# First weight chunk in pieces of one k-tile, with the transposed input beside the weights

## The chip, the cores and the metric

The kernel runs on one core of a Trainium2 chip. The metric is the device time of one execution in microseconds (us), lower is better. Every time below is from runs of the kernel before the change or from the trace of one profiled execution of it.

## What is computed

One hybrid layer on an input `x` of 256 rows by 1024 columns in float32: a gated feed-forward block, a mixer (causal depthwise convolution beside attention over 16 heads), and a second gated feed-forward block. The change touches the beginning of the first block alone:

```
def rms_norm(x, g):
    xf = x.astype(jnp.float32)
    y = xf * lax.rsqrt(jnp.mean(xf * xf, axis=-1, keepdims=True) + EPS)
    return (y * g.astype(jnp.float32)).astype(x.dtype)

def swiglu(h, w_gate, w_up, w_down):
    return (jax.nn.silu(h @ w_gate) * (h @ w_up)) @ w_down

    x = x + 0.5 * swiglu(rms_norm(x, ffn1_norm), ffn1_w_gate, ffn1_w_up, ffn1_w_down)
```

## The kernel before, in words

Every product `h @ w` is cut into chunks of 512 columns of `w` (256 for the last columns). A chunk has 8 k-tiles: 128 rows of `w` each, against 128 features of `h`. The method `gemm` does one chunk. It loads pieces of up to two k-tiles into `raw` (a ring of 5 tiles), and for each piece ScalarE (ACT) writes `hi`, the weights rounded to a type that TensorE (PE) multiplies in one pass, and VectorE (DVE) writes `lo`, the rest that the rounding left. The activations exist in the same two halves, `hTh` and `hTl`. For each k-tile and each of the two halves `t` of the rows there are then three matmuls of 128x512: `hi` by `hTh`, `lo` by `hTh`, `hi` by `hTl`. So one chunk is 8 x 2 x 3 = 48 matmuls, which add up in two PSUM banks `acc` (a ring of 3 banks).

The first block's `ffn` takes chunks in pairs: chunk one is gate columns (`g`), chunk two the up columns (`u`) that belong to them. `sg`, the silu of `g`, and `av`, the product of `sg` and `u`, need the reciprocal root of the mean of squares, `rs`. It is applied after the product, so that the matmuls need only `x` transposed times the gain, which is what `hTh` and `hTl` hold.

In the first chunk the function `start` loads `x` transposed (`x0` with the gains for k-tile 0, `xT` for the others, in pieces of 1, 2, 2 and 2 k-tiles) in turn with the weight pieces (1, 1, 2, 2 and 2 k-tiles). ACT makes `hTh`, DVE makes `hTl`, and GpSimd (POOL) squares each k-tile of `xT` and adds the squares into `sq`. After the chunk PE adds `sq` over the partitions (`tr<-ones,sq`), DVE makes `ms` of it, and POOL `rs`. After chunk two `load_rest` issues the loads of the constants `cst` and of `x` in its natural layout, which is first read at 166 us.

All loads are issued by one queue, SyncE's (SP), in program order. A load into a `raw` tile waits until `lo` of the piece that lay there before is written, and all loads behind it wait too. The order of instructions on each engine is fixed when the program is built; each engine works through its own list and waits at semaphores. Two more PSUM tiles, `cv`, are used before the change by the convolution alone, in the middle of the kernel.

Of the kernel before, what the change touches and what calls it, by code (L numbers as in the profile page):

```python
# [17 lines left out]
P = 128  # L18
# [26 lines left out]
class Build:  # L45
# [14 lines left out]
    def acc(self):  # L60
        return self.ps.tile([P, CH], F32, tag="acc", name="acc", bufs=3)

    def tr(self):
        return self.ps.tile([P, CH], F32, tag="tr", name="tr", bufs=3)
# [31 lines left out]

    def gemm(self, w, c, n, kt, ah, al, pump=0, pool=0.0, first=False, split_k=None,
             side=None, before=None):

# [8 lines left out]
        for kp in sizes:  # L108
            ahead = before(k0) if before is not None else None
# [3 lines left out]
            with self.tc.issue_after(ahead.ins) if ahead else nullcontext():  # L113
                self.last_dma = nc.sync.dma_start(
                    raw[:, : kp * n].rearrange("p (k n) -> p k n", n=n), w(c, k0, kp)
                )
            step = 1 if first else 2
            for s in range(0, kp, step):
                e = min(s + step, kp)
                self.share += pool  # L120
                pool_lo = self.share >= 1.0
                if pool_lo:
                    self.share -= 1.0
                self.split(
                    raw[:, s * n : e * n], hi[:, s * n : e * n], lo[:, s * n : e * n], pool_lo
                )
            for t in range(2):
# [83 lines left out]

    def ffn(self, wgu, wd, hT, rstd_of, x, emit, tail=None, before=None, after=None):

# [8 lines left out]
        for i, n in enumerate(widths):  # L222
            last = i == len(widths) - 1
            if not last:
                if before is not None and i == 0:
                    g = self.gemm(
                        wgu, c, n, KD, ah, al, first=True, split_k=(1, 1), before=before
                    )
                else:
                    g = self.gemm(wgu, c, n, KD, ah, al)  # L230
                c += 1
                if rstd is None:
# [8 lines left out]
                u = self.gemm(wgu, c, n, KD, ah, al)  # L241
                c += 1
                if i == 0 and after is not None:
                    after()
# [54 lines left out]
    def conv(self, uT, tiles):  # L299
# [3 lines left out]
        for c0 in tiles:  # L303
            accs = [self.ps.tile([P, S], F32, tag="cv", name="cv", bufs=2) for _ in range(2)]
            for j in range(TAPS - 1, -1, -1):
# [195 lines left out]
    def run(self):  # L501
        nc, tc, io = self.nc, self.tc, self.io
        cst = self.cst = self.const.tile([P, C_ALL], F32, name="cst")
        x = self.big("x")
        xT = self.big("xT")
        hTh, hTl = self.big("hTh", F32R), self.big("hTl", F32R)

        def w_of(name, kt, n_of=lambda c: CH, off_of=None):
            t = io[name]

            def f(c, k0, kp):
                n = n_of(c)
                base = c * P * kt * CH
                a = t[base : base + P * kt * n].rearrange("(p k n) -> p k n", p=P, n=n)
                return a[:, k0 : k0 + kp, :]

            return f
# [7 lines left out]
        for _ in range(WARM):  # L525
            nc.tensor.matmul(wps[:, :P], idle, idle, start=True, stop=True)
        xT_d = io["xT"]

        sq = self.big("sq")
        self.ones = self.const.tile([P, 2], F32, name="ones")  # L530
        nc.vector.memset(self.ones, 1.0)

        def start(k0):

            if k0 == 0:
                dma = nc.sync.dma_start(x0, io["x0"])
                ks = (0,)
            elif k0 == 1:
                dma = nc.sync.dma_start(xT[:, S : 2 * S], xT_d[:, S : 2 * S])
                ks = (1,)  # L540
            else:
                sl = slice(k0 * S, (k0 + 2) * S)
                dma = nc.sync.dma_start(xT[:, sl], xT_d[:, sl])
                ks = (k0, k0 + 1)
            for j in ks:
                g = x0[:, j : j + 1]
                sl = slice(j * S, (j + 1) * S)
                src = xT[:, sl] if j else x0[:, KD:]
                nc.gpsimd.tensor_tensor(sq[:, sl], src, src, ALU.mult)
                if j:  # L550
                    nc.gpsimd.tensor_tensor(sq[:, :S], sq[:, :S], sq[:, sl], ALU.add)
                nc.scalar.activation(hTh[:, sl], src, AF.Copy, scale=g)
                nc.vector.scalar_tensor_tensor(
                    hTl[:, sl], src, g, hTh[:, sl].bitcast(F32), ALU.mult, ALU.subtract
                )
            return dma

        x0 = self.const.tile([P, KD + S], F32, name="x0")
# [8 lines left out]
        def ss_tile(name):  # L567
            return self.tmp.tile([P, 4], F32, tag="ss", name=name, bufs=2)

        def rstd_x():  # L570

            sums = self.tr()
            for t in range(2):
                nc.tensor.matmul(
                    sums[:, t : t + 1], sq[:, t * P : (t + 1) * P], self.ones[:, :1],
                    start=True, stop=True,
                )
            return self.rsqrt_mean(sums[:, :2], D, 2)

        def load_rest():  # L580
            with tc.issue_after(self.last_dma.ins):
                nc.sync.dma_start(cst, io["cst"])
# [10 lines left out]
        def emit_into(dst, src):  # L593
# [6 lines left out]

        self.ffn(
            w_of("w1gu", KD), w_of("w1d", KF), (hTh, hTl), rstd_x, x, emit_into(x1, x),
            self.residual_T(x1, ss1, h1h, h1l, C_GM), before=start, after=load_rest,
        )
# [209 lines left out]
```

## Time and profile before

| | |
|---|---|
| time, median of 3 runs | 655.03 us (653.30 to 655.46) |
| time of the profiled execution | 653.98 us |
| span in its trace | 652.2 us, so 1.8 us lie around it |
| PE busy | 640.5 us, 98% of the span |
| DVE busy, ACT busy | 413.1 us (63%), 342.6 us (53%) |
| matmuls in the trace | 2956 |

The span runs from the first instruction to the last one in the trace. A busy share says how much of the span an engine had work under way; for PE the ends of matmuls are modelled, so it can be busy and yet slow. Times inside the kernel are counted from the start of the span.

### The profile page before, as it was taken

The numbers are of one execution on the slowest core, as the hardware profiler recorded it, in microseconds if no ns is written. First come the engines' busy times: TensorE is split into PE (matmuls) and PEld (weight loads), VectorE is DVE, ScalarE is ACT, GpSimd is POOL, SyncE is SP. The second block draws the span as 40 slices with busy tenths as digits, with TensorE's granted clock in tenths as the row PEclk, the third lists the DMA queues.
The fourth block names the chain that finished last, engine by engine and source line by source line (L and its number), as shares of the span: only waits on it lengthen the run. The fifth ranks groups of instructions, "written<-read, shape, count | busy, mean of one in ns | idle before, by whom it ended". The sixth has DMA issues, their size and how long they took to land.

```text
span 652.2 us, 8131 instructions
## 1 busy us (share of the span) xinstructions
PE 640.5 (98%) x2956; PEld 519.8 (80%) x2956; DVE 413.1 (63%) x664; ACT 342.6 (53%) x512; POOL 132.5 (20%) x80
## 2 busy tenths in 40 slices
PE   7999999999999999999999999999999999999997
PEld 5788888888888888877777777788888888888886
DVE  5764636455532399999989874775754546455541
ACT  5543545354534645668665685943654535454330
POOL 6300000000025667847744400000000000000000
PEclk8999999999999999999999999999999999999999
DMA  8865655647565556444454433365655666656740
GB/s 275 315 224 164 193 193 173 216 132 233 163 213 163 183 175 219 144 153 134 156 162 130 162 124 102 130 207 179 197 171 182 193 194 182 189 162 204 206 124 32
DMA packets 33000, 114.98 MB, mean 176 GB/s; under 512 B 3648, under 2 KB 5056, under 8 KB 32960
## 3 DMA queue, kind: packets, MB, share of 16 engines
q1 hardware_dynamic: 32960, 114.46, 54.8%
q8 instruction: 23, 0.38, 0.3%
q14 instruction: 17, 0.14, 0.1%
HBM read 113.40 MB, written 1.05 MB: 175 GB/s over the span
## 4 chain that ended last, share of the span: by engine, by line
PE 90%; DVE 3%; ACT 3%; DMA 1%; issue 1%; SPq 0%; DVEq 0%; ACTq 0%
PE acc L134 28%; PE acc L133 28%; PE acc L135 28%; PE tr L178 2%; PE tr L423 1%; DMA raw<-w1gu 1%; PE tr L481 1%; DVE cv L317 1%; DVE lo L93 1%; ACT hi L91 1%; PE tr L466 1%; ACT gate L686 1%; ACT pr L445 0%; DVE hxn L385 0%; PE tr L397 0%
## 5 line engine op out<-in xcount | busy, mean ns | idle before, releaser
L91 ACT CAST hi<-raw 128x1024 fp32r<-128x1024 f32 (+1 forms) x216 | 222.9, 1037 | 242.1 <-PE acc L135 217.3
L93 DVE TENSOR_TENSOR lo<-raw,hi 128x1024 fp32r<-128x1024 f32 (+1 forms) x174 | 217.2, 1253 | 182.1 <-ACT hi L91 177.2
L93 POOL TENSOR_TENSOR lo<-raw,hi 128x1024 fp32r<-128x1024 f32 x42 | 100.9, 2421 | 219.4 <-ACT hi L91 219.2
L317 DVE SCALAR_TENSOR_TENSOR cv<-uT,cst,cv 128x255 f32<-128x255 f32 (+26 forms) x240 | 94.4, 463 | 0.1
L134 PE MATMUL acc<-lo,h1h 128*128 128x512 f32 x224 | 88.3, 394 | 0.0
L135 PE MATMUL acc<-hi,h1l 128*128 128x512 f32 x224 | 87.5, 394 | 0.0
L133 PE MATMUL acc<-hi,h1h 128*128 128x512 f32 x224 | 87.2, 394 | 0.0
L133 PE MATMUL acc<-hi,hTh 128*128 128x512 f32 x176 | 68.8, 397 | 2.9 <-ACT hi L91 2.9
L134 PE MATMUL acc<-lo,hTh 128*128 128x512 f32 x176 | 69.9, 397 | 0.7 <-DVE lo L93 0.7
L133 PE MATMUL acc<-hi,h2h 128*128 128x512 f32 x176 | 69.2, 393 | 0.0
L135 PE MATMUL acc<-hi,hTl 128*128 128x512 f32 x176 | 69.0, 393 | 0.0
L133 PE MATMUL acc<-hi,aTh 128*128 128x512 f32 x176 | 68.7, 391 | 0.0
L135 PE MATMUL acc<-hi,aTl 128*128 128x512 f32 x176 | 68.5, 389 | 0.0
L134 PE MATMUL acc<-lo,aTh 128*128 128x512 f32 x176 | 68.5, 389 | 0.0
L134 PE MATMUL acc<-lo,h2h 128*128 128x512 f32 x176 | 68.5, 390 | 0.0
L135 PE MATMUL acc<-hi,h2l 128*128 128x512 f32 x176 | 67.2, 390 | 0.0
L133 PEld LDWEIGHTS acc<-hi,h1h 128*128 128x128 f32 x224 | 42.1, 188 | 10.4 <-issue 1.3
L134 PEld LDWEIGHTS acc<-lo,h1h 128*128 128x128 f32 x224 | 42.1, 188 | 9.6 <-issue 0.7
L135 PEld LDWEIGHTS acc<-hi,h1l 128*128 128x128 f32 x224 | 42.1, 188 | 8.5 <-issue 0.3
L133 PEld LDWEIGHTS acc<-hi,hTh 128*128 128x128 f32 x176 | 33.4, 191 | 10.3 <-ACT hi L91 3.6
L134 PEld LDWEIGHTS acc<-lo,hTh 128*128 128x128 f32 x176 | 33.5, 190 | 8.9 <-DVE lo L93 2.2
L155 POOL TENSOR_TENSOR rs<-ms,neghalf 128x8 f32<-128x8 f32 (+2 forms) x13 | 17.2, 1324 | 109.7 <-DVE ms L153 109.4
(131 smaller groups left out, 783.8 us busy)
## 6 DMA issues: line engine op xcount, KB each, us to landing
raw<-w_in SPq DMA_DIRECT2D x56, 512.0 KB, 3.5
raw<-w2gu SPq DMA_DIRECT2D x44, 512.0 KB, 4.4
raw<-w1gu SPq DMA_DIRECT2D x43, 512.0 KB, 5.0
raw<-w1d SPq DMA_DIRECT2D x22, 512.0 KB, 4.2
raw<-w2d SPq DMA_DIRECT2D x22, 512.0 KB, 4.3
raw<-w_attn SPq DMA_DIRECT2D x8, 512.0 KB, 4.0
raw<-w_conv SPq DMA_DIRECT2D x8, 512.0 KB, 3.5
raw<-w_out SPq DMA_DIRECT2D x8, 512.0 KB, 4.5
```

The costliest lines, as they stand in the source:

```text
L91: nc.scalar.copy(hi, raw)
L93: ins = eng.tensor_tensor(lo, raw, hi.bitcast(F32), ALU.subtract)
L133: nc.tensor.matmul(o, ah(k, t), wh, start=st, stop=False)
L134: nc.tensor.matmul(o, ah(k, t), wl, start=False, stop=False)
L135: nc.tensor.matmul(o, al(k, t), wh, start=False, stop=sp)
L155: nc.gpsimd.tensor_tensor(r, ms, self.neghalf[:, :width], ALU.pow)
L178: nc.tensor.transpose(ps[:, j * S + t * P : j * S + (t + 1) * P], src(t, j), self.ident)
L317: nc.vector.scalar_tensor_tensor(o, i, w, o, ALU.mult, ALU.add)
L423: nc.tensor.matmul(ps[q][:, t * P : t * P + (t + 1) * P], qT[r, b * S + t * P : b * S + (t + 1) * P], kT[r, b * S : b * S + (t + 1) * P], ...
L466: nc.tensor.transpose(ps[:, i * P : (i + 1) * P], pr[:, o : o + P], self.ident)
L481: nc.tensor.matmul(ps[q * HD : (q + 1) * HD, kt * P : S], v[:, kt * D + h * HD : kt * D + (h + 1) * HD], pT[:, o : o + n], start=kt == 0, ...
L686: last = nc.scalar.activation(g[:, sl], g[:, sl], AF.Sigmoid)
```

## The change

`gemm_first` replaces `gemm` for chunk one. It loads eight pieces of one k-tile. Piece 0 is `x0` (as before) and 256 KB of weights, now contiguous in memory. Pieces 1 to 7 are one load each of 384 KB, a row of which holds 512 weights and the 256 columns of `x` transposed; both parts lie in the `raw` tile. Each piece takes a `raw`, a `hi` and a `lo` tile of its own. The host lays out a new input `w1f` for this; `w1gu` begins with chunk two. The products of chunk one add up in the two `cv` banks, so that chunk two finds all three `acc` banks free. POOL's squares, the tile `sq` and PE's sums are gone. In their place `x` is loaded in its natural layout right behind the last piece of chunk two, ACT squares it with a running sum (`sum_squares`, four instructions, `junk`), and `rms` makes `rs` after chunk two instead of after chunk one.

```
+    def gemm_first(self, x0, w0, rest, hT):
...
+        acc = [self.cv(), self.cv()]
...
+        for k in range(KD):
...
+            if k == 0:
+                nc.sync.dma_start(x0, self.io["x0"])
+                nc.sync.dma_start(raw[:, :CH], w0)
+                xk = x0[:, KD:]
+            else:
+                self.last_dma = nc.sync.dma_start(raw[:, : CH + S], rest[:, k - 1, :])
+                xk = raw[:, CH : CH + S]
...
+            nc.scalar.activation(hTh[:, sl], xk, AF.Copy, scale=g)
+            nc.vector.scalar_tensor_tensor(
+                hTl[:, sl], xk, g, hTh[:, sl].bitcast(F32), ALU.mult, ALU.subtract
+            )
+            self.split(raw[:, :CH], hi[:, :CH], lo[:, :CH], False)
+            for t in range(2):
+                o, st, sp = acc[t], k == 0, k == KD - 1
+                nc.tensor.matmul(o, ah(k, t), hi[:, :CH], start=st, stop=False)
+                nc.tensor.matmul(o, ah(k, t), lo[:, :CH], start=False, stop=False)
+                nc.tensor.matmul(o, al(k, t), hi[:, :CH], start=False, stop=sp)
...
                 if rstd is None:
+                    if first is not None:
+                        u = self.gemm(wgu, c, n, KD, ah, al)
                     rstd = rstd_of()
...
         def rstd_x():
 
-            sums = self.tr()
-            for t in range(2):
-                nc.tensor.matmul(
-                    sums[:, t : t + 1], sq[:, t * P : (t + 1) * P], self.ones[:, :1],
-                    start=True, stop=True,
-                )
-            return self.rsqrt_mean(sums[:, :2], D, 2)
...
+                nc.sync.dma_start(cst, io["cst"])
+            for t in range(2):
+                for c in range(2):
+                    self.sum_squares(x, ss0, t, c)
+            return self.rms(ss0)
```

On SP's queue, at the start of the program before the change, the loads of `xT` and of weights alternate (`x_92` is the tile `x0`), and the second row from the end is `cst`:

```order
L536 DMA x_92<-x 128x264
L114 DMA raw<-w1gu 128x512
L539 DMA xT<-xT 128x256
L114 DMA raw<-w1gu 128x512
L543 DMA xT<-xT 128x512
L114 DMA raw<-w1gu 128x1024
L543 DMA xT<-xT 128x512
L114 DMA raw<-w1gu 128x1024
L543 DMA xT<-xT 128x512
L114 DMA raw<-w1gu 128x1024 x5
L582 DMA cst<-cst 128x290
L583 DMA x<-x 128x2x1024
```

The same stretch of SP's queue with the change (`x_88` is the tile `x0`):

```order
L111 DMA x_88<-x 128x264
L112 DMA raw<-w1f 128x512
L115 DMA raw<-w1f 128x768 x7
L145 DMA raw<-w1gu 128x1024 x4
L575 DMA x<-x 128x2x1024
L579 DMA cst<-cst 128x290
L145 DMA raw<-w1gu 128x1024 x36
```

Nine loads bring chunk one where there were ten, and `x` stands between the weights of chunk two and those of chunk three, as before, but is now waited for.

On ACT, from the last k-tiles of chunk one into chunk three, before:

```order
L552 ACTIVATE hTh<-xT,x_92 128x256 x2
L91 CAST hi<-raw 128x512 x2
L91 CAST hi<-raw 128x1024 x4
L237 ACTIVATE sg<-acc,rs 128x512 x2
L91 CAST hi<-raw 128x1024 x7
```

And with the change:

```order
L119 ACTIVATE hTh<-raw,x_88 128x256
L94 CAST hi<-raw 128x512
L94 CAST hi<-raw 128x1024 x4
L187 ACTIVATE junk,ss_102<-x 128x512 x4
L94 CAST hi<-raw 128x1024 x2
L264 ACTIVATE sg<-cv,rs 128x512 x2
L94 CAST hi<-raw 128x1024 x5
```

Four squares of `x` have come in behind the four casts of chunk two, and the two `sg` stand two casts later. From chunk three's transposes on, each engine's list is the same in both kernels.

## Rows read from the trace of the kernel before

**Rows 1.** The page, part 1: span, and busy time of PE.

```profile
span 652.2 us, 8131 instructions
PE 640.5 (98%) x2956; PEld 519.8 (80%) x2956; DVE 413.1 (63%) x664; ACT 342.6 (53%) x512; POOL 132.5 (20%) x80
```

**Rows 2.** Busy time by stretch: chunk one, chunk two, a later pair of chunks.

```profile
core 0: us, PE busy (x) PEld busy (x) DVE busy (x) ACT busy (x) POOL busy (x), PEclk, DMA share, GB/s
4.79:22.41 17.62, 14.02 (x49) 10.04 (x49) 14.70 (x17) 10.69 (x18) 12.19 (x14) 0.90 0.85 294
22.41:33.28 10.87, 10.87 (x51) 9.05 (x50) 6.28 (x7) 5.78 (x7) 1.62 (x1) 1.00 0.96 352
...
64.11:86.79 22.68, 22.68 (x106) 18.84 (x105) 12.22 (x13) 10.56 (x12) 0.00 (x0) 1.00 0.57 186
```

**Rows 3.** Timeline, PE: start, duration, instruction; chunk one to the start of chunk two.

```profile
4.79 1.01 PE L133 MATMUL acc<-hi,hTh 128*128 128x512 f32 x2
...
13.41 0.63 PE L133 MATMUL acc<-hi,hTh 128*128 128x512 f32 x1
...
13.84 0.63 PE L134 MATMUL acc<-lo,hTh 128*128 128x512 f32 x1
...
22.18 0.40 PE L135 MATMUL acc<-hi,hTl 128*128 128x512 f32 x1
...
23.33 0.40 PE L135 MATMUL acc<-hi,hTl 128*128 128x512 f32 x1
```

**Rows 4.** Timeline, ACT: start, duration; in brackets the idle time and its releaser.

```profile
4.12 0.62 ACT L91 CAST hi<-raw 128x512 fp32r<-128x512 f32 x1 [0.71 <-DMA raw<-w1gu]
...
5.59 0.62 ACT L91 CAST hi<-raw 128x512 fp32r<-128x512 f32 x1 [0.45 <-DMA raw<-w1gu]
9.42 0.91 ACT L552 ACTIVATE hTh<-xT,x 128x256 fp32r<-128x256 f32 x2 [3.21 <-DMA xT<-xT]
10.65 1.14 ACT L91 CAST hi<-raw 128x512 fp32r<-128x512 f32 x2 [0.32 <-DMA raw<-w1gu]
...
13.00 1.14 ACT L91 CAST hi<-raw 128x512 fp32r<-128x512 f32 x2 [0.40 <-DMA raw<-w1gu]
...
14.91 1.14 ACT L91 CAST hi<-raw 128x512 fp32r<-128x512 f32 x2
```

**Rows 5.** Busy time by stretch inside chunk one (columns as in rows 2).

```profile
8.38:11.32 2.94, 0.00 (x1) 0.00 (x1) 1.26 (x3) 1.58 (x4) 1.85 (x3) 1.00 1.00 367
...
12.24:15.65 3.41, 3.26 (x8) 2.58 (x9) 3.41 (x5) 3.01 (x7) 3.41 (x5) 0.50 0.95 377
```

**Rows 6.** Groups by form, 0 to 24 us: count, busy us, mean ns, idle before.

```profile
L93 DVE TENSOR_TENSOR lo<-raw,hi 128x512 fp32r<-128x512 f32 x8 | 8.3, 1072 | 0.9 <-ACT hi L91 0.8
...
L553 DVE SCALAR_TENSOR_TENSOR hTl<-xT,x,hTh 128x256 fp32r<-128x256 f32 x7 | 5.5, 817 | 2.8 <-ACT hTh L552 2.8
L91 ACT CAST hi<-raw 128x512 fp32r<-128x512 f32 x8 | 4.7, 616 | 1.9 <-DMA raw<-w1gu 1.9
L91 ACT CAST hi<-raw 128x1024 fp32r<-128x1024 f32 x4 | 4.2, 1054 | 2.6 <-DMA raw<-w1gu 2.6
...
L93 DVE TENSOR_TENSOR lo<-raw,hi 128x1024 fp32r<-128x1024 f32 x3 | 3.5, 1212 | 0.0
L552 ACT ACTIVATE hTh<-xT,x 128x256 fp32r<-128x256 f32 x7 | 3.2, 499 | 3.2 <-DMA xT<-xT 3.2
L155 POOL TENSOR_TENSOR rs<-ms,neghalf 128x2 f32<-128x2 f32 x1 | 1.6, 1622 | 3.0 <-DVE ms L153 3.0
```

**Rows 7.** Timeline, DVE: two instructions with POOL idle for most of them.

```profile
3.45 0.48 DVE L553 SCALAR_TENSOR_TENSOR hTl<-x,hTh 128x256 fp32r<-128x256 f32 x1 [2.41 <-ACT hTh L552]
...
6.46 0.68 DVE L93 TENSOR_TENSOR lo<-raw,hi 128x512 fp32r<-128x512 f32 x1
```

**Rows 8.** DMA issues, 0 to 20 us: count, KB each, median us to landing.

```profile
raw<-w1gu SPq DMA_DIRECT2D x7, 512.0 KB, 9.0
x<-x SPq DMA_DIRECT2D x1, 1024.0 KB, 6.6
```

**Rows 9.** All squares of the residual, ACT: duration in ns, minimum, median, maximum.

```profile
L161 ACT ACTIVATE junk<-x x8: 622/630/633, 167.8 to 464.4; 128x512 f32<-128x512 f32 x8
```

More of the change, by code (lines that the diff above doesn't have):

```diff
@@ L61, in acc, with cv @@
         return self.ps.tile([P, CH], F32, tag="acc", name="acc", bufs=3)
+    def cv(self):
+        return self.ps.tile([P, CH], F32, tag="cv", name="cv", bufs=2)
     def tr(self):
@@ L95, in split, with gemm @@
             self.anchor = ins
-    def gemm(self, w, c, n, kt, ah, al, pump=0, pool=0.0, first=False, split_k=None,
-             side=None, before=None):
+    def gemm_first(self, x0, w0, rest, hT):
+        nc = self.nc
+        acc = [self.cv(), self.cv()]
+        hTh, hTl = hT
+        ah, al = self.parts(*hT)
+        for k in range(KD):
+            raw = self.wp.tile([P, KP * CH], F32, tag="raw", name="raw", bufs=RAW_BUFS)
+            hi = self.wp.tile([P, KP * CH], F32R, tag="hi", name="hi", bufs=HI_BUFS)
+            lo = self.wp.tile([P, KP * CH], F32R, tag="lo", name="lo", bufs=LO_BUFS)
+            if k == 0:
[5 more added lines that the diff above has]
+                xk = raw[:, CH : CH + S]
+            g = x0[:, k : k + 1]
+            sl = slice(k * S, (k + 1) * S)
+            nc.scalar.activation(hTh[:, sl], xk, AF.Copy, scale=g)
[8 more added lines that the diff above has]
+                nc.tensor.matmul(o, al(k, t), hi[:, :CH], start=False, stop=sp)
+        return acc
+    def gemm(self, w, c, n, kt, ah, al, pump=0, pool=0.0, split_k=None, side=None):
         nc = self.nc
@@ L108, in gemm @@
         for kp in sizes:
-            ahead = before(k0) if before is not None else None
             raw = self.wp.tile([P, KP * CH], F32, tag="raw", name="raw", bufs=RAW_BUFS)
@@ L112, in gemm @@
             lo = self.wp.tile([P, KP * CH], F32R, tag="lo", name="lo", bufs=LO_BUFS)
-            with self.tc.issue_after(ahead.ins) if ahead else nullcontext():
-                self.last_dma = nc.sync.dma_start(
-                    raw[:, : kp * n].rearrange("p (k n) -> p k n", n=n), w(c, k0, kp)
-                )
[L117 to L126, printed above, removed]
+            self.last_dma = nc.sync.dma_start(
+                raw[:, : kp * n].rearrange("p (k n) -> p k n", n=n), w(c, k0, kp)
+            )
+            self.share += pool
+            pool_lo = self.share >= 1.0
+            if pool_lo:
+                self.share -= 1.0
+            self.split(raw[:, : kp * n], hi[:, : kp * n], lo[:, : kp * n], pool_lo)
             for t in range(2):
@@ L209, in parts, with ffn @@
         return ap(hi), ap(lo)
-    def ffn(self, wgu, wd, hT, rstd_of, x, emit, tail=None, before=None, after=None):
+    def ffn(self, wgu, wd, hT, rstd_of, x, emit, tail=None, first=None):
         nc = self.nc
@@ L224, in ffn @@
             if not last:
[L225 to L228, printed above, removed]
+                if first is not None and i == 0:
+                    g = first()
                 else:
@@ L240, in ffn @@
                     sg.append(s)
-                u = self.gemm(wgu, c, n, KD, ah, al)
+                if u is None:
+                    u = self.gemm(wgu, c, n, KD, ah, al)
                 c += 1
-                if i == 0 and after is not None:
-                    after()
                 up = [u[t][:, :n] for t in range(2)]
@@ L303, in conv @@
         for c0 in tiles:
-            accs = [self.ps.tile([P, S], F32, tag="cv", name="cv", bufs=2) for _ in range(2)]
+            accs = [self.cv()[:, :S] for _ in range(2)]
             for j in range(TAPS - 1, -1, -1):
@@ L526, in run @@
             nc.tensor.matmul(wps[:, :P], idle, idle, start=True, stop=True)
[L527 to L556, printed above, removed]
         x0 = self.const.tile([P, KD + S], F32, name="x0")
@@ L568, in ss_tile, with first @@
             return self.tmp.tile([P, 4], F32, tag="ss", name=name, bufs=2)
-        def rstd_x():
-            sums = self.tr()
-            for t in range(2):
-                nc.tensor.matmul(
-                    sums[:, t : t + 1], sq[:, t * P : (t + 1) * P], self.ones[:, :1],
-                    start=True, stop=True,
-                )
-            return self.rsqrt_mean(sums[:, :2], D, 2)
-        def load_rest():
+        def first():
+            return self.gemm_first(
+                x0, io["w1f"][: P * CH].rearrange("(p n) -> p n", n=CH),
+                io["w1f"][P * CH :].rearrange("(p k n) -> p k n", p=P, n=CH + S), (hTh, hTl),
+            )
+        ss0 = ss_tile("ss0")
+        def rstd_x():
             with tc.issue_after(self.last_dma.ins):
-                nc.sync.dma_start(cst, io["cst"])
                 nc.sync.dma_start(
@@ L601, in run @@
         self.ffn(
-            w_of("w1gu", KD), w_of("w1d", KF), (hTh, hTl), rstd_x, x, emit_into(x1, x),
-            self.residual_T(x1, ss1, h1h, h1l, C_GM), before=start, after=load_rest,
+            w_of("w1gu", KD, first=1), w_of("w1d", KF), (hTh, hTl), rstd_x, x, emit_into(x1, x),
+            self.residual_T(x1, ss1, h1h, h1l, C_GM), first=first,
         )
```

20 lines of the change are left out of this document (11 added, 9 removed).

## Prediction, made before the changed kernel ran

> **What bounds the kernel now.** I began with the page: PE is busy for 98% of the span [rows 1], so nothing is gained off PE's path, and what is left to gain on it is where PE waits or runs slowly. The view of busy time by stretch shows where. In the middle of the first block a pair of chunks takes 22.68 us, PE busy throughout [rows 2]; chunk two takes 10.87 us, again without a pause. Chunk one, with the same 48 matmuls, takes 17.62 us, from 4.79 to 22.41 [rows 2]. So 17.62 - 10.87 = 6.75 us are lost there, and that is all that an edit to chunk one can win on PE, but for what it moves out of the stretch that follows.
>
> Three causes share these 6.75 us, and the finer stretches and timelines show them. First, data: k-tiles 2 and 3 are not there. ACT is idle for 3.21 us until `xT` lands at 9.42, and casts the weights at 10.65 [rows 4]; PE does nothing from 8.38 to 11.32 [rows 5]. Second, the clock: after that pause the granted clock is 0.50 from 12.24 to 15.65 [rows 5], which is 1.2 of 2.4 GHz. Matmuls start 0.43 us apart there (13.41 and 13.84 [rows 3]), where 10.87 / 48 = 0.23 us is normal; eight of them stand in that stretch, 8 x 0.20 = 1.6 us. Third, DVE: it is busy for 14.70 of the 17.62 us, while POOL works for 12.19 of them [rows 2]. A `lo` of 512 columns takes 1072 ns on average and an `hTl` 817 [rows 6], but 0.68 and 0.48 us when POOL is idle for all or most of them [rows 7]. So the last weights are there by 14.91, when ACT casts them without a wait [rows 4], and yet chunk one ends only at 22.41.
>
> **Removed.** POOL's fifteen squares and sums go. They are on no path of their own, but DVE gets back 8 x (1.07 - 0.68) + 7 x (0.82 - 0.48) = 5.5 us. DVE's work for a k-tile falls to 0.48 + 0.68 = 1.16 us, ACT's is 0.50 + 0.62 = 1.12 us [rows 6, 7], PE's 6 x 0.23 = 1.36 us. None of the three then needs longer than PE. PE's sums go too: the third matmul of chunk two starts at 23.33, 0.92 us after the first at 22.41, where two steps are 0.45. That third matmul is the mark by which I compare, since from it on both kernels have the same 46 matmuls to do in chunk two.
>
> **Added and moved in chunk one.** Bytes first: x0 with 132 KB, 256 KB, and seven times 384 KB are the same 3076 KB as before, in 9 loads instead of 10. I therefore take the landings that the trace shows for the same bytes: k-tile 0 at 4.12, k-tile 1 at 5.6, k-tiles 2 and 3 at 10.65, 4 and 5 at 13.0, 6 and 7 at 14.9 [rows 4], and for the first of each pair the middle between its neighbours: 8.1, 11.8, 14.0. This may be too late, since behind chunk one's bytes two pieces of chunk two already share the queue before the change, and with the change they can't. It may be too early, since a piece now holds a `raw` tile of its own: pieces 5, 6 and 7 wait until `lo` of pieces 0, 1 and 2 is written. By my landings `lo` 2 is written at 8.1 + 0.50 + 0.62 + 0.05 + 0.68 = 9.95, so piece 7 has 5 us to land. The nearest rows are 512 KB pieces with a median of 9.0 us in a full queue, and 1024 KB in 6.6 us behind fewer [rows 8]. I take 14.9 and keep the 9.0 for the other end.
>
> K-tile 1 costs a little: its `hTh` now waits for the weights' load too, so its cast ends at 5.6 + 1.12 = 6.7 instead of 6.2. PE is in the matmuls of k-tile 0 until about then, so I cost it at nothing; without that cover it would be 0.5 us.
>
> The tail: ACT has a small backlog, since four k-tiles land in 3.1 us and take 1.12 us each: 11.8 + 1.12 = 12.9, then 13.0 + 3 x 1.12 = 16.4 for the last cast. `lo` is there 0.73 us later at 17.1, and the last four matmuls end at 17.1 + 0.9 = 18.0. Chunk one then ends at 18.0 instead of 22.41.
>
> **Chunk two's first piece** is late next. Its load waits for `lo` 3, written at 10.65 + 1.85 = 12.5. Behind 14.9 its 512 KB take 512 KB / 352 GB/s = 1.5 us (rate from chunk two [rows 2]): it lands at 16.4. Its cast, 1.05 us, ends at 17.45, its `lo`, 1.21 us [rows 6], at 18.7. PE does two matmuls of it from 18.0, and the third waits until 18.7. Against 23.33 [rows 3] that is 4.6 us earlier. The three other pieces wait for `lo` 4 to 6 in turn and come about 1.2 us apart, faster than the 2.7 us in which PE uses one. Chunk two ends at 18.7 + 46 x 0.227 = 29.1.
>
> **The squares of x.** ACT waits for `x` in front of chunk three's casts. `x` is issued behind chunk two's last piece, which waits for `lo` 6 at about 16.0, so near 16.5; with 6.6 us to land [rows 8] it is there at 23.1. Four squares of 0.63 us [rows 9] end at 25.7, chunk three's first cast at 26.7, its `lo` at 28.0, the second cast at 27.8. POOL's `rs` takes 1.62 us [rows 6], to about 27.7; the two `sg`, 0.6 to 0.7 us each, end near 29.1, and the third cast at 30.2, where PE needs it at 29.1 + 12 x 0.227 = 31.8. All of it is hidden behind chunk two, by about 1.3 us at the tightest place, the `lo` of chunk three's first piece. If `x` lands later than 24.3, each us costs one. Loading `cst` later costs nothing, since its reader comes far behind it.
>
> Everything behind chunk three keeps its order, and PE is the bound of it, so the 4.6 us stay. On the profiled execution: 653.98 - 4.6 = 649.4 us (span 647.6). That execution lies 1.05 us below the median of the runs shown, so the forecast for a median is 655.03 - 4.6 = 650.4 us.
>
> **The rivals.** *Best case:* the loads run at the 352 GB/s of chunk two from the start and PE is the only limit: 4.79 + 48 x 0.227 + about 0.6 of waits = 16.3, third matmul at 16.7, a gain of 6.6 us: 648.4. Against it: 294 GB/s is the mean over chunk one [rows 2], and the 3.21 us wait is there in the trace.
>
> *The chain of buffers binds.* Piece 7, issued at 9.95, takes the 9.0 us of [rows 8] and lands at 18.95; chunk two's first piece, issued at 12.5, lands at 21.5, its `lo` is written at 23.8. That is 0.5 us later than 23.33: 655.5, no change. For it: five `raw` tiles now hold 5 k-tiles where they held 8. Against it: a 9.0 us landing had up to 3 MB ahead of it, and now at most four pieces of 384 KB can be.
>
> *x is late.* At a landing of 27 instead of 24.3 the gain falls by 2.7 to 1.9 us: 653.1. For it: the load of `x` stands behind four pieces of 512 KB. Against it: before, it also stood behind such pieces, and took 6.6 us.
>
> *Slower: the clock falls and stays low in chunk one.* PE's work is now cut into eight parts of 1.36 us with a wait for a load in front of each. If the granted clock were 0.50 for all of chunk one, as it was from 12.24 to 15.65 after one long pause [rows 5], 48 matmuls at 0.43 us take 20.6 us, to 25.4; two more at 0.43 put the third matmul at 26.3, 3.0 us later than 23.33: 658.0. The Trainium skill, page "TensorE: Matmul & The Clock Gate", section "HAM oscillation — how this bites in real kernels", tells of a kernel that waits for a load at every k-tile and starts each one with a cold clock; by that rule the change would come out on this side. In the trace the clock fell only after PE stood still for the whole 2.94 us from 8.38 to 11.32 [rows 5], and by my landings no pause is longer than about 1 us (k-tile 1's matmuls end at about 8.2, k-tile 2's cast at 9.2), so I give it little. It decides once more than 4.6 / 0.20 = 23 matmuls beyond those that wait anyway run at the low level; one spell such as the one seen costs at most 1.6 us.
>
> **How the numbers follow.** Forecast, a gain of 3 to 6.6 us: 0.70. x late or a cold spell, a gain of 2 to 3 us: 0.14. Buffers bind, within 0.3% (about 2 us, what a measurement of this kernel tells from no change): 0.10. Slower by more than that: 0.06. So faster 0.84, same 0.10, slower 0.06. The range runs from 648.0, the best case less 0.4 for the spread of medians, to 653.8, a gain of 1.2; it leaves out most of the buffers' case and the slow clock.
>
> **What would show it.** Right: no squares on POOL before 20 us, `lo` of 512 columns near 0.68 us, chunk two's third matmul near 18.7, ACT's first `junk` near 23, and no idle PE between 18.7 and 35. The landings are wrong if k-tile 7's cast starts beyond 17 or before 13. The clock is wrong if the granted clock stays 0.50 for more than one spell before 20 us. `x` is wrong if ACT's wait for it ends behind 24.3 and PE then waits for a cast of chunk three. The prediction fails if chunk two's third matmul starts behind 22, or if a stall of 2 us or more stands behind it.

## The result, and the profile after

The changed kernel takes 649.23 us in the median of five runs (647.71 to 650.88), the kernel before 654.85 us in the five runs beside them (653.30 to 655.46). The ratio is 0.9917, with a 95% interval of 0.9892 to 0.9941: 5.4 to 5.6 us less, by the ratio and by the medians. In a second comparison, told below, it was 649.09 beside 653.67, a ratio of 0.9927. The forecast was 650.4 within 648.0 to 653.8.

The profiled execution took 647.71 us, the fastest of the five. Its page, part 1, beside [rows 1]:

```profile
span 645.9 us, 8120 instructions
...
PE 637.7 (99%) x2952; PEld 518.4 (80%) x2952; DVE 408.4 (63%) x664; ACT 345.2 (53%) x520; POOL 118.6 (18%) x65
```

The span is 6.3 us shorter than before. The same two stretches as in [rows 2], with the same columns:

```profile
4.79:22.41 17.62, 17.62 (x75) 13.83 (x75) 12.90 (x19) 11.09 (x18) 0.00 (x0) 1.00 0.97 337
22.41:33.28 10.87, 10.87 (x50) 8.97 (x49) 7.42 (x9) 9.31 (x16) 0.71 (x1) 1.00 0.92 332
```

In the 17.62 us in which PE had worked for 14.02 at a mean clock of 0.90, it now works all the time at 1.00, and 75 matmuls stand in the trace where there were 49. POOL does nothing there. On PE's timeline chunk one gives way to chunk two (L159) at 16.32, and the third matmul of chunk two starts at 16.83, where it was 23.33 [rows 3]: 6.50 us earlier.

```profile
16.09 0.39 PE L128 MATMUL cv<-hi,hTl 128*128 128x512 f32 x1
16.32 0.61 PE L159 MATMUL acc<-hi,hTh 128*128 128x512 f32 x2
16.83 0.50 PE L160 MATMUL acc<-lo,hTh 128*128 128x512 f32 x1
```

So the whole difference of the spans, 6.3 us, lies in front of that matmul, and only 0.2 us are given back behind it. Of the 6.50 us, 5.97 are chunk one's own (11.65 us from its first product to chunk two's, where it took 17.62), 0.12 an earlier start, and 0.41 the way from chunk two's first product to its third, from which PE's sums are gone. ACT's timeline tells when the data came. Rows for k-tile 3 (`hTh`), k-tile 7 (`hTh` and cast), chunk two's first two pieces, the first square of `x` and the first cast of chunk three, beside [rows 4]:

```profile
8.04 0.51 ACT L119 ACTIVATE hTh<-raw,x 128x256 fp32r<-128x256 f32 x1 [0.75 <-DMA raw<-w1f]
...
11.84 0.51 ACT L119 ACTIVATE hTh<-raw,x 128x256 fp32r<-128x256 f32 x1
12.26 0.61 ACT L94 CAST hi<-raw 128x512 fp32r<-128x512 f32 x1
14.46 1.05 ACT L94 CAST hi<-raw 128x1024 fp32r<-128x1024 f32 x1 [1.60 <-DMA raw<-w1gu]
16.96 1.05 ACT L94 CAST hi<-raw 128x1024 fp32r<-128x1024 f32 x1 [1.45 <-DMA raw<-w1gu]
...
22.47 0.64 ACT L187 ACTIVATE junk<-x 128x512 f32<-128x512 f32 x1 [1.43 <-DMA x<-x]
...
24.95 1.99 ACT L94 CAST hi<-raw 128x1024 fp32r<-128x1024 f32 x2
```

The 3.21 us wait of [rows 4] is gone, the longest in chunk one's k-tiles 2 to 7 is 0.75, and k-tile 7 is taken up at 11.84 without a wait. The view by form gives DVE's prices, 0 to 24 us, beside [rows 6]:

```profile
L96 DVE TENSOR_TENSOR lo<-raw,hi 128x512 fp32r<-128x512 f32 x8 | 5.5, 691 | 0.8 <-ACT hi L94 0.7
...
L120 DVE SCALAR_TENSOR_TENSOR hTl<-raw,x,hTh 128x256 fp32r<-128x256 f32 x7 | 3.4, 483 | 0.9 <-ACT hTh L119 0.9
```

`lo` fell from 1072 to 691 ns and `hTl` from 817 to 483, close to the durations of [rows 7].

### The profile page after: what moved, and what is told of

It reads as the page before. It is cut to its first block, busy times and chain, and to the rows that moved or that the text cites. A ratio compares the mean times of both kernels' runs of the same rounds, so it can differ in the third digit from the quotient of the medians.

```text
span 645.9 us, 8120 instructions
## 1 busy us (share of the span) xinstructions
PE 637.7 (99%) x2952; PEld 518.4 (80%) x2952; DVE 408.4 (63%) x664; ACT 345.2 (53%) x520; POOL 118.6 (18%) x65
## 4 chain that ended last, share of the span: by engine, by line
PE 93%; DVE 3%; ACT 3%; issue 1%; DVEq 0%; ACTq 0%
PE acc L159 28%; PE acc L160 28%; PE acc L161 28%; PE tr L204 2%; PE tr L449 1%; PE tr L507 1%; DVE cv L343 1%; DVE lo L96 1%; PE tr L492 1%; ACT gate L683 1%; PE cv L126 1%; PE cv L127 1%; PE tr L551 1%; PE cv L128 1%; ACT pr L471 0%
## 5 line engine op out<-in xcount | busy, mean ns | idle before, releaser
L96 DVE TENSOR_TENSOR lo<-raw,hi 128x1024 fp32r<-128x1024 f32 (+1 forms) x174 | 214.6, 1236 | 181.3 <-ACT hi L94 176.6
L159 PE MATMUL acc<-hi,h1h 128*128 128x512 f32 x224 | 87.3, 395 | 0.0
L159 PE MATMUL acc<-hi,h2h 128*128 128x512 f32 x176 | 69.1, 393 | 0.0
L159 PE MATMUL acc<-hi,aTh 128*128 128x512 f32 x176 | 68.7, 391 | 0.0
L160 PE MATMUL acc<-lo,hTh 128*128 128x512 f32 x160 | 62.5, 391 | 0.0
L161 PE MATMUL acc<-hi,hTl 128*128 128x512 f32 x160 | 62.2, 390 | 0.0
L159 PE MATMUL acc<-hi,hTh 128*128 128x512 f32 x160 | 62.0, 391 | 0.0
L159 PEld LDWEIGHTS acc<-hi,h1h 128*128 128x128 f32 x224 | 42.1, 188 | 10.4 <-issue 1.3
L181 POOL TENSOR_TENSOR rs<-ms,neghalf 128x8 f32<-128x8 f32 (+2 forms) x13 | 16.3, 1255 | 129.9 <-DVE ms L179 129.6
L161 PEld LDWEIGHTS acc<-hi,aTl 128*128 128x128 f32 x176 | 33.0, 188 | 6.8
L159 PEld LDWEIGHTS acc<-hi,h2h 128*128 128x128 f32 x176 | 33.1, 188 | 6.8
```

The costliest lines, as they stand in the source:

```text
L96: ins = eng.tensor_tensor(lo, raw, hi.bitcast(F32), ALU.subtract)
L159: nc.tensor.matmul(o, ah(k, t), wh, start=st, stop=False)
L160: nc.tensor.matmul(o, ah(k, t), wl, start=False, stop=False)
L161: nc.tensor.matmul(o, al(k, t), wh, start=False, stop=sp)
L181: nc.gpsimd.tensor_tensor(r, ms, self.neghalf[:, :width], ALU.pow)
```

## The experiments

The main theory: the loads (pause and cold clock) and DVE's slow instructions are two limits that lie one over the other, and both must go. Its rivals: DVE, slowed by POOL, is the limit alone, or the pause and the clock are the loss alone. Later questions were what in the loads made the pause, and what bounds the changed kernel now. Ratios are to the kernel before on the same chip, in five rounds each. The mark is the start of chunk two's third matmul: 23.33 before, 16.83 after.

### Only the squares gone

The kernel before without POOL's squares and sums of k-tiles 1 to 7; the mean of squares is then over 128 of 1024 features.

```
-                nc.gpsimd.tensor_tensor(sq[:, sl], src, src, ALU.mult)
-                if j:
-                    nc.gpsimd.tensor_tensor(sq[:, :S], sq[:, :S], sq[:, sl], ALU.add)
+                if j == 0:
+                    nc.gpsimd.tensor_tensor(sq[:, sl], src, src, ALU.mult)
```

> The kernel before, with POOL's squares of k-tiles 1 to 7 and the additions left out, so that the mean of squares is taken over 128 of the 1024 features; loads, banks and PE's sums as before. Theory A (the pause for loads and the cold spell behind it set the end of chunk one, DVE's slowness adds only the two short waits for lo of 0.3 us each): a gain of 0.5 to 1.5 us, 653.3 to 654.4 against 654.85, the pause before k-tile 2 still near 3 us and the granted clock 0.50 for one spell. Rival B (DVE slowed by POOL is what kept chunk one from ending with its loads, as the third cause in the prediction says): lo of 512 columns near 0.68 us and a gain of 3 to 5 us, 650 to 652. Rival C (the late landings were those of one execution): no pause in this trace, and a gain of 5 us or more.

Measured: 652.38 us, ratio 0.9977 [0.9965, 0.9988]; mark at 21.92. `lo` took 686 ns, so DVE was free, but PE stood still for k-tile 2 and ran at half the clock after it. The row of PE's timeline, and the stretch by windows (columns as in rows 2):

```profile
11.29 0.73 PE L133 MATMUL acc<-hi,hTh 128*128 128x512 f32 x2 [2.66 <-ACT hi L91]
```

```profile
12.76:16.17 3.41, 3.41 (x9) 2.65 (x9) 3.41 (x8) 3.21 (x7) 0.00 (x0) 0.50 0.98 380
```

The pause stays without POOL's squares, so they don't cause it, and in this execution a fast DVE alone gains 1.4 us at the mark, or about 2 without the 0.58 us by which the first product started later (5.37 instead of 4.79; the scheduler put PE's sums in front of it). The mean granted clock of a whole execution (1.000 is full speed throughout) says more: one spell like this one lowers it to 0.997. Eight of the twelve executions lie at 0.997 or below, with a median of 652.49 us, and four at 0.999, with a median of 650.40. Of the kernel before beside them, 18 executions at 0.996 or 0.997 have a median of 653.32 and seven at 1.000 one of 653.29. So a lower clock goes with 2.1 us where DVE is fast and with nothing where it is slow: the one limit hides the other.

### Only the loads changed

The kernel before with the changed kernel's loads; POOL's squares and PE's sums, the `acc` banks and the late load of `x` stay.

```
+            self.last_dma = nc.sync.dma_start(raw[:, : CH + S], rest[:, k - 1, :])
+            xk = raw[:, CH : CH + S]
...
+            nc.gpsimd.tensor_tensor(sq[:, sl], xk, xk, ALU.mult)
+            if k:
+                nc.gpsimd.tensor_tensor(sq[:, :S], sq[:, :S], sq[:, sl], ALU.add)
```

> The changed kernel's loads of chunk one alone: w1f in pieces of one k-tile with x transposed beside the weights. POOL's squares, PE's sums, the acc banks, the order of rs and the late load of x are as before the change. Theory A (the new loads remove the pause, all else is small): chunk two's third matmul at 17 to 19.5, a gain of 4 to 6 us, 649 to 651. Rival B (POOL slows DVE to about 1.9 us for a k-tile, 8 x 1.9 = 15 us from 3 us on, so DVE is the limit): third matmul near 20 or later, a gain of 2 to 3.5 us, 651.5 to 653. Rival D (a raw tile that now also waits for POOL's square holds up pieces 5 to 7): a gain under 1.5 us.

Measured: 652.06 us, 0.9977 [0.9968, 0.9986]; mark at 21.49. No long pause and no cold clock, but PE waited for `lo` in seven of eight k-tiles, once every 1.9 us. Waits of PE, 0 to 33 us (waited for; us in total, times, longest), and DVE's `lo` by form:

```profile
PE acc L131 <- DVE lo L96: 1.9, 7, 0.4
```

```profile
L96 DVE TENSOR_TENSOR lo<-raw,hi 128x512 fp32r<-128x512 f32 x8 | 8.5, 1067 | 0.4 <-ACT hi L94 0.4
```

Without the pause DVE's 1.07 + 0.82 = 1.89 us for a k-tile set the pace: from 8.25 us to the end of chunk one it works without a gap.

```profile
8.25:20.58 12.33, 10.81 (x41) 6.96 (x40) 12.33 (x14) 7.90 (x14) 10.38 (x12) 1.00 0.77 240
```

So it isn't waiting for `raw` tiles that POOL's squares still hold, the third case of the expectation. The gain is 1.84 us at the mark, less than either of the first two cases had. Neither limit was the loss alone.

### Squares put back into the changed kernel

POOL's squares and sums, their result unused.

```
+            nc.gpsimd.tensor_tensor(sq[:, sl], xk, xk, ALU.mult)
+            if k:
+                nc.gpsimd.tensor_tensor(sq[:, :S], sq[:, :S], sq[:, sl], ALU.add)
```

> The changed kernel with POOL's squares and additions of x transposed put back beside it, unused. Theory A (loads decide, DVE has room): lo of 512 columns rises to about 1.0 us, PE waits for lo in several k-tiles, but chunk two's third matmul comes at most 1.5 us later than with the change, 649 to 651. Rival B (DVE at 1.9 us for a k-tile becomes the limit of chunk one): third matmul 2.5 to 4 us later, 652 to 653.5.

Measured: 651.54 us, 0.9971 [0.9961, 0.9980]; mark at 21.04, 4.2 us behind the changed kernel's. The only edit is work whose result nobody reads, and it takes back most of the gain:

```profile
L96 DVE TENSOR_TENSOR lo<-raw,hi 128x512 fp32r<-128x512 f32 x8 | 8.6, 1078 | 1.3 <-ACT hi L94 1.3
```

### New loads and no squares, the rest as before

The second experiment with POOL's squares left out but for k-tile 0's; the mean is again over 128 of 1024 features. PE's sums and the `acc` banks stay.

```
-            nc.gpsimd.tensor_tensor(sq[:, sl], xk, xk, ALU.mult)
-            if k:
-                nc.gpsimd.tensor_tensor(sq[:, :S], sq[:, :S], sq[:, sl], ALU.add)
+            if k == 0:
+                nc.gpsimd.tensor_tensor(sq[:, sl], xk, xk, ALU.mult)
```

> The changed kernel's loads and no squares on POOL but that of k-tile 0 (so the mean of squares is taken over 128 of the 1024 features), with acc banks, PE's sums and the late load of x as before the change: the two halves of the change without the cv banks and without the wait for x. Theory A (new loads and a fast DVE are each worth little alone and the whole gain together): 647.5 to 649.5, and chunk two's third matmul near 17.5. Rival V (the free acc banks that cv leaves to chunk two are part of the gain): 1.5 us or more slower than with the change, 650 or more, with PE waiting for a bank in chunk two.

Measured: 649.66 us, 0.9937 [0.9925, 0.9950]; mark at 17.84, 1.0 us behind the changed kernel's. Both halves together make nearly all of the gain. What is left at the mark: the scheduler now put PE's sums in front of the first product (it starts at 5.37 instead of 4.67), and PE waited 0.76 us for chunk two's first `lo`; no wait for a bank is named. The profiled execution, 650.44 us, holds besides a spell at half the clock at 412 us, long after the mark (see the clock, below), so here the mark tells more than the time. The `cv` banks and the late squares are thus a way to have the mean of squares without POOL, and worth little by themselves.

### Old loads in the changed kernel

The other half of the second experiment: no squares on POOL, `cv` banks, late squares of `x`, but the ten loads of before.

```
-                self.last_dma = nc.sync.dma_start(raw[:, : CH + S], rest[:, k - 1, :])
-                xk = raw[:, CH : CH + S]
+                with self.tc.issue_after(self.last_dma.ins):
+                    xd0 = nc.sync.dma_start(self.xT[:, xs], xd[:, xs])
+            with self.tc.issue_after(xd0.ins):
+                self.last_dma = nc.sync.dma_start(
+                    raw[:, : kp * CH].rearrange("p (k n) -> p k n", n=CH), wd[:, k0 : k0 + kp, :]
+                )
```

> The changed kernel with the loads of before: x transposed in pieces of 1, 2, 2 and 2 k-tiles of its own, in turn with weights of 1, 1, 2, 2 and 2 k-tiles; no squares on GpSimd, products in the two cv banks, x squared by ScalarE late. It is the other half of e2_loads_only. Theory (the old list of loads itself makes the pause, by pieces and x apart together): hTh of k-tile 2 starts near 9.1 us, TensorE stands still for 2.5 to 3 us before k-tile 2, the granted clock then falls to 0.50 for about 3 us, and chunk two's third matmul starts near 21.5: a gain of 1 to 2 us over before. Rival (the loads were slow for another reason, squares or buffers among them): no pause of over 1 us, third matmul near 17.5, a gain of 5 us or more, as e5_pairs and e6_x_apart.

Measured: 650.82 us, 0.9963 [0.9949, 0.9976]; mark at 21.24. PE's timeline and the stretch of the cold clock by windows:

```profile
10.60 0.73 PE L136 MATMUL cv<-hi,hTh 128*128 128x512 f32 x2 [2.15 <-ACT hi L94]
```

```profile
12.12:15.54 3.42, 3.42 (x10) 2.64 (x9) 2.91 (x7) 2.93 (x6) 0.00 (x0) 0.50 1.02 401
```

In all three traces with this list of loads the pause and the cold spell are there, whatever else is in the kernel; pieces 5 to 10 of that list wait for no buffer. Its mark lies 4.41 us behind the changed kernel's: 2.15 of pause, some 1.6 of cold clock (the price worked out in the prediction), and 0.66 of smaller things. This execution took 651.85 us, 1.0 above the median: seven of the twelve have a mean clock of 0.999 or 1.000 and a median of 650.50, so the old list doesn't bring a cold spell each time, and without one it still stays 1.5 us or more behind the changed kernel's executions without one (medians of 648.6 and 649.0). The pause was 2.15 here, 2.66 in the first experiment and 2.94 before, so the theory's 2.5 to 3 us was a little high.

### What in the list makes the pause

Three edits of the changed kernel. First, rows of `w1f` 32 KB apart in memory, as in the list of before, instead of 21 KB:

```
-                io["w1f"][P * CH :].rearrange("(p k n) -> p k n", p=P, n=CH + S), (hTh, hTl),
+                io["w1f"][P * CH :].rearrange("(p k n) -> p k n", p=P, n=2 * CH)[:, :, : CH + S],
```

> The changed kernel with one size different: in memory the rows of w1f lie 32 KB apart instead of 21 KB (each partition's seven pieces padded to eight pieces of 4 KB, of which 3 KB are loaded as before). Theory L (rows of w1gu 16 KB apart and of xT 8 KB apart were what slowed the loads before the change): k-tile 3 is cast at 10 or later, a pause of 1.5 us or more on PE, and the gain falls to 2 to 4 us, 651 to 653. Rival Q (it was the number, size and order of the loads): landings within 0.7 us of those with the change, 648.5 to 650.

Measured: 647.97 us, 0.9920 [0.9907, 0.9933]; mark at 16.98. This distance of the rows makes no difference. Second, `x` still beside the weights, but pieces of 1, 1, 2, 2 and 2 k-tiles, the pairs in tiles of their own, chunk two's loads behind them:

```
+        pieces = [(0, 1), (1, 1), (2, 2), (4, 2), (6, 2)]
+            raw = self.pairs[k0 // 2 - 1] if kp == 2 else self.wp.tile(
```

> The changed kernel with the pieces of chunk one as before the change, 1, 1, 2, 2 and 2 k-tiles, but x still beside the weights in the same rows (768 KB for a pair, in tiles of their own, so that no piece of chunk one waits for a buffer). Theory P (a k-tile can only begin when its whole piece is there, and pairs make k-tile 2 wait for two): PE pauses 1 to 3 us before k-tile 2, a gain of 2 to 4.5 us, 649 to 651.5. Rival S (the many small loads of x apart from the weights slowed the queue before the change): no pause over 1 us, a gain of 5 to 6 us, 647.5 to 648.5.

Measured: 648.53 us, 0.9926 [0.9914, 0.9939]; mark at 17.59, no wait of PE named. Third, pieces of one k-tile, but `x` in loads of its own (16 loads in place of nine):

```
-                self.last_dma = nc.sync.dma_start(raw[:, : CH + S], rest[:, k - 1, :])
+                nc.sync.dma_start(raw[:, CH : CH + S], xr[:, k - 1, :])
+                self.last_dma = nc.sync.dma_start(raw[:, :CH], wr[:, k - 1, :])
```

> The changed kernel with pieces of one k-tile, but x transposed in an input and loads of its own, 128 KB before each 256 KB of weights: 16 loads for chunk one instead of 9. Theory S (small loads of x apart from the weights slow the queue, in rows of 1 KB): landings late as before the change, k-tile 3 cast at 9.5 or later, a gain of 1 to 4 us, 649.5 to 652.5. Rival P (it is the size of a piece alone): no pause of PE over 1 us, 647.5 to 649.

Measured: 648.97 us, 0.9932 [0.9919, 0.9945]; mark at 18.29, two waits of PE of 0.3 and 0.5 us. Neither pairs nor `x` apart brings the pause back; both together do, as the experiment above shows. So neither part of the new layout can be credited alone: either would have been nearly enough (648.53 and 648.97 us, where the changed kernel has 649.23 and 649.09). Why the two together are slow isn't settled. In that kernel the view of DMA shows 195, 160, 119 and 225 GB/s in the half microseconds from 4.5 to 6.5, where the changed kernel has 393, 381, 252 and 369; SP's timeline has one issue that took 1.62 us there. In the first experiment, where the dip is deepest, the DMA engines were not full, busy for 0.35 to 0.71 of the time from 5 to 6.5 us, but in this kernel's lowest half microsecond they were busy for 0.94 of it. Two rows of the windows of the first experiment:

```profile
5.00:5.50 0.50, 0.50 (x4) 0.50 (x3) 0.50 (x2) 0.29 (x2) 0.00 (x0) 1.00 0.35 102
5.50:6.00 0.50, 0.50 (x3) 0.40 (x3) 0.50 (x3) 0.50 (x1) 0.00 (x0) 1.00 0.71 74
```

These things are seen; none is shown to be the cause.

### What bounds the changed kernel

An additional load of 1 MB in front of `x`:

```
+                nc.sync.dma_start(
+                    spare.rearrange("p (t d) -> p t d", t=2),
+                    io["x"].rearrange("(t p) d -> p t d", p=P),
+                )
```

> The changed kernel with one more load of 1 MB, into a tile that nobody reads, in front of the load of x. x then lands some 2.8 us later, near 25.3. Theory T (in the trace with the change the squares end at 25.0 and the lo of chunk three's first piece at 27.2, just when PE wants it, so nothing is left to hide a later x): 2 to 3 us slower than with the change, 650 to 651.5, and PE waits for a cast or a lo of chunk three. Rival H (1.3 us of cover, as the prediction has it): 1 to 1.8 us slower. Rival N (x is not on the path): within 0.7 us of the change.

Measured: 651.63 us, 0.9969 [0.9957, 0.9981]. The squares began at 27.05 instead of 22.47, and PE then waited for chunk three. Waits of PE, 0 to 33 us:

```profile
PE acc L159 <- ACT hi L94: 1.4, 1, 1.4
...
PE acc L160 <- DVE lo L96: 0.9, 2, 0.8
```

Of these, 1.42 and 0.76 us stand at 30.6 and 31.9. Chunk two's mark was at 18.46 in that execution, 1.6 behind the changed kernel's own trace, which gave `x` as much more cover. What the late `x` cost is read from the mark to chunk three's first product with `lo`, here and in the changed kernel:

```profile
31.86 0.50 PE L160 MATMUL acc<-lo,hTh 128*128 128x512 f32 x1 [0.76 <-DVE lo L96]
```

```profile
27.64 0.39 PE L160 MATMUL acc<-lo,hTh 128*128 128x512 f32 x1
```

That is 13.40 us against 10.81, so `x` 4.6 us later costs 2.6, of which the named waits are 2.2. The load of `x` is close to being a limit: 4.6 - 1.6 - 2.6 leaves 0.4 us of cover. Then the reverse: pieces 5 to 7 in tiles of their own, so that no load of chunk one waits for a `lo`.

```
+            raw = self.own[k - 5] if k >= 5 else self.wp.tile(
+                [P, KP * CH], F32, tag="raw", name="raw", bufs=RAW_BUFS
+            )
```

> The changed kernel with tiles of their own for pieces 5, 6 and 7, so that no load of chunk one waits for a lo, and chunk two's loads and x are issued earlier. Theory (x's load has practically no cover left, so its delay is the next limit and may be part of the spread between runs): squares of x start near 20 us instead of 22.5, by 1 us or more of cover, chunk two's third matmul stays near 16.8, and the time is 0 to 0.7 us under the changed kernel's, with less spread. Rival (earlier loads of chunk two take bandwidth from chunk one's last pieces): k-tile 7 lands later than 11.9 us, TensorE waits in chunk one, and chunk two's third matmul starts behind 17.5: 0.5 us or more slower than the changed kernel.

Measured: 647.70 us (647.62 to 648.11), 0.9912 [0.9896, 0.9927]; squares at 20.29, mark at 17.24. `x` came as the theory said, k-tile 3 a little late (ACT waited 0.97 us for it). But the ratio's interval overlaps that of the changed kernel. So both ran once more, in one comparison:

> The changed kernel as it is, beside e12 on the same chip. Theory (x has no cover in it, so a late x costs time in some executions): median 0.5 us or more above e12's, and a spread of over 2 us, as its first five runs had (647.71 to 650.88). Rival (the spread belonged to the chip of that day, and x's cover is worth nothing): both medians agree within 0.4 us and both spreads are alike.

> The kernel of e10_own_tiles again, beside the changed kernel on the same chip. Theory (cover for x): 0.5 us or more under the changed kernel, spread of under 0.6 us as before (647.62 to 648.11). Rival: within 0.4 us of the changed kernel, or slower by the 0.4 us by which its chunk two starts later.

Measured: the changed kernel 649.09 us (648.84 to 650.02), 0.9927 [0.9912, 0.9941]; with own tiles 647.60 us (647.54 to 649.23), 0.9909 [0.9892, 0.9927]. The intervals overlap and one of the five runs with own tiles is as slow as the others'; the medians lie 1.5 us apart in favour of own tiles. A small gain is likely and not proven. My expectation put it on the cover of `x`, and the trace of the changed kernel's second execution says otherwise: no wait stands at chunk three. Its chunk two's mark is at 18.01, on ACT's and on PE's timeline:

```profile
15.64 1.05 ACT L94 CAST hi<-raw 128x1024 fp32r<-128x1024 f32 x1 [2.31 <-DMA raw<-w1gu]
```

```profile
18.01 0.50 PE L160 MATMUL acc<-lo,hTh 128*128 128x512 f32 x1 [0.53 <-DVE lo L96]
```

The first piece of chunk two was late there. SP's queue waited for buffers, 3.9 us inside chunk one (L115, three pieces; 0 to 25 us) and then for chunk two's, and issued that piece's load at 9.62:

```profile
SPq L145 <- DVE lo L96: 8.0, 8, 2.4
SPq L115 <- DVE lo L96: 3.9, 3, 1.7
```

```profile
9.62 3.32 SPq L145 DMA_DIRECT2D raw<-w1gu  x4
```

The changed kernel's first trace has waits of the same kind and the issue no earlier, yet the cast at 14.46:

```profile
9.82 3.32 SPq L145 DMA_DIRECT2D raw<-w1gu  x4
```

So the waits alone don't tell these two executions apart; from issue to cast it took 6.0 us in the one and 4.6 in the other, and why isn't shown. With own tiles the load is issued at 5.31, the cast of that piece starts at 13.14, the mark is at 16.94:

```profile
5.31 4.29 SPq L147 DMA_DIRECT2D raw<-w1gu  x4
```

```profile
13.14 1.05 ACT L94 CAST hi<-raw 128x1024 fp32r<-128x1024 f32 x1 [0.82 <-DMA raw<-w1gu]
```

The spans of the two profiled executions, 647.0 and 645.8 us, differ by 1.2, their marks by 1.07. So what own tiles removed between these two is the wait for buffers: the load is out 4.3 us earlier, and a slow landing is covered. The spread of the first five runs is another matter: the longest, 650.88, has a mean clock of 0.997 and the other four 1.000, so a cold spell is very likely in it; those four still lie 1.8 us apart (647.71 to 649.48), and no run shows why.

## Why the prediction was right, and where its size was off

**What bounds the kernel.** Right: the gain lies in front of the mark, and 5.97 of chunk one's 6.75 us came back.

**Three causes.** All three are there, but they don't share the 6.75 us as parts of a sum. Taking away DVE's slowness alone brings 1.41 us at the mark (first experiment) or 2.09 (old loads in the changed kernel); taking away the pause alone brings 1.84 (second experiment); both bring 6.50. In the kernel before, the cold clock was covered by DVE. PE, after its slow stretch, still had to wait for a `lo` in the last k-tiles:

```profile
19.98 0.50 PE L134 MATMUL acc<-lo,hTh 128*128 128x512 f32 x1 [0.32 <-DVE lo L93]
```

Its executions are as long at a mean clock of 1.000 as at 0.997, as the first experiment's comparison shows, and once DVE is fast the cold clock is on the path. The prediction didn't work out what one removal would be worth without the other.

**DVE's price.** Right: 0.48 + 0.69 = 1.17 us for a k-tile against 1.16 forecast. Putting the squares back restores 1.08 and 0.89.

**The landings.** This is the term that was mis-sized: "I therefore take the landings that the trace shows for the same bytes". Same bytes did not land at the same times. K-tile 7 was taken up at 11.84, not 14.9, chunk two's first piece at 14.46, not 16.4, and chunk one ended at 16.32, not 18.0. Its cast at 12.26 lies before 13, which the prediction itself had named as the sign that its landings are wrong. The old landings had the list's own slow stretch in them, and 14.9 was never a landing: in [rows 4] ACT casts there without a wait, so the data had come earlier. The case that happened in the profiled execution is the rival *best case*, 16.3 and 16.7 for the end of chunk one and the mark, measured 16.32 and 16.83; its 648.4 us is for a median and makes 647.4 for the profiled execution, measured 647.71. Its premise was an even rate, and the argument against it (294 GB/s, the 3.21 us wait) took two symptoms of the old list for a property of the bytes. The median, 649.23, lies between the two, and so does the second trace, with k-tile 7 at 12.32, chunk two's first piece at 15.64 and the mark at 18.01. That the forecast's 4.6 us came so close to the 5.6 and 4.6 by the medians of the two comparisons is in part luck: its late landings come from the old list, and the late piece of the second trace has another origin.

**Buffers bind.** This rival was priced too high and is real in kind. SP's waits in the changed kernel's first trace, and its issues (count, KB each, median us to landing):

```profile
SPq L115 <- DVE lo L96: 3.2, 3, 1.3
```

```profile
raw<-w1f SPq DMA_DIRECT2D x7, 384.0 KB, 4.1
```

The 9.0 us landing that it was built on did not come. But SP waited for three `lo` inside chunk one, which kept the issue of chunk two's first piece until 9.8 and 9.6 us; where that piece then took 6.0 us to its cast, PE waited 0.53 us for its `lo`.

**x.** The landing was forecast at 23.1, measured 22.47; the cover was forecast at 1.3 us. But the limit of 24.3 belonged to a mark at 18.7. With the mark 1.9 us earlier it moves to about 22.4, and the landing stood right on it; the load of 1 MB in front of `x` leaves 0.4 us of cover. POOL's `rs` took 0.71 us instead of the 1.62 of [rows 6], with DVE idle for most of it.

**The clock.** The rival did not occur in the two traces of the changed kernel. The granted clock is 1.00 in both stretches above, although PE's eight parts each need a load; the waits that the trace names are short, at most 0.2 us in chunk one in the second trace. The Trainium skill, page "TensorE: Matmul & The Clock Gate", section "HAM oscillation — how this bites in real kernels", tells of a kernel that waits about 3 to 5 us for a load at every k-tile and restarts cold each time. In this case 2.15, 2.66 and 2.94 us of standing still were each followed by a clock of 0.50, while seven waits of 0.2 to 0.4 us in the second experiment were not. The prediction gave the rival little because by its landings no wait in chunk one was longer than about 1 us, and there that held.

The length of a wait doesn't decide alone, however. At about 410 us PE waits 1.3 and then 0.3 us. In the trace of new loads and no squares it then ran at half the clock from 412.2 us:

```profile
410.26 0.50 PE L162 MATMUL acc<-hi,u2h 128*128 128x512 f32 x1 [1.28 <-ACT u2h L394]
...
411.79 0.60 PE L164 MATMUL acc<-hi,u2l 128*128 128x512 f32 x1 [0.34 <-DVE u2l L395]
```

```profile
412.20:415.18 2.98, 2.98 (x8) 2.32 (x7) 2.98 (x5) 2.98 (x6) 0.00 (x0) 0.50 0.75 247
```

In the changed kernel's trace the same two waits were followed by no such spell:

```profile
409.15 0.50 PE L159 MATMUL acc<-hi,u2h 128*128 128x512 f32 x1 [1.29 <-ACT u2h L391]
...
410.68 0.50 PE L161 MATMUL acc<-hi,u2l 128*128 128x512 f32 x1 [0.34 <-DVE u2l L392]
```

```profile
411.02:414.02 3.00, 3.00 (x15) 2.47 (x14) 3.00 (x5) 3.00 (x6) 0.00 (x0) 1.00 0.77 264
```

No run shows what decides between the two. Such spells reach the times: in each of three sets of five, the changed kernel's two and own tiles' second, the longest execution (650.88, 650.02 and 649.23 us) is the one with a mean clock of 0.997. No trace shows where in the kernel theirs stand. So the prediction's cold spell, "a gain of 2 to 3 us", was the right kind of thing to price, and one such execution in five moves a median little.

## What to carry to other kernels

When two limits lie one over the other, their losses don't add up to the whole: cost each removal with the other one still in place. Landings were a property of the list of loads here, not of its bytes; when the list changes, take the old ones as a late bound and work out the early bound from the best rate that the trace shows. An engine that nobody waits for can still set the pace by slowing its neighbour, which shows as the same instruction at two durations. And compare two executions at a mark close behind the change as well as by their whole time: a spell of low clock elsewhere moved the time by some 2 us here.

## What was not expected of the hardware

Ten loads in pairs with `x` apart let the rate fall for some 2 us, to 90, 74 and 119 GB/s in half a microsecond in the three kernels with that list, with the DMA engines busy for only 0.35 to 0.71 of the deepest dip (but for 0.94 of it in the kernel with 119); the same bytes in lists of 6, 9 or 16 loads fell no lower than 178 between 3 and 6.5 us. The distance of rows in memory, 21 or 32 KB, made no difference. POOL's squares lengthen both of DVE's operations here, `lo` from 0.69 to 1.07 us and `hTl` from 0.48 to 0.82, and POOL's own 128x2 `rs` fell from 1.62 to 0.71 us when DVE was idle for most of it. The clock of 0.50 came when PE was at work again, not in the pause: with the old loads in the changed kernel PE started at 10.60 and the granted clock was 0.50 from 12.12. And the same wait of 1.3 us was followed by half the clock in one execution and not in another.
